# One gather ahead of the overflow loop, the last expert's weights loaded early, and one memory's keys and values moved into the first mixture's tail

## The chip, the cores and the metric

The kernel runs on one core of a Trainium2 chip. The metric is the device time of one execution in microseconds (us), as the median of the runs. A matrix product runs on TensorE (PE), elementwise work on VectorE (DVE), ScalarE (ACT) and GpSimd (POOL). SyncE (SP) issues the plain DMA loads, and POOL issues the indirect ones (gathers and scatters by a list of rows). Each engine works through its own instructions in order, and they wait for one another by semaphores.

## The reference

Two blocks of two layers each work on 512 tokens of width 1024. The change touches the second block only. Each of its two layers mixes the tokens, normalises, sends each token to 2 of 16 experts, and normalises again:

```python
def memory_branch(mq, mem, w_mem_kv):          # mem: 256 x 1024, w_mem_kv: 1024 x 1024
    kv = jnp.einsum('bmd,de->bme', mem, w_mem_kv)
    mk, mv = jnp.split(kv, 2, axis=-1)         # 4 heads of 128
    ...
    s = jnp.einsum('bshd,bmhd->bhsm', q, mk) * (MEM_HEAD_DIM ** -0.5)
    p = jax.nn.softmax(s, axis=-1)
    return jnp.einsum('bhsm,bmhd->bshd', p, mv)

def second_block(x, mem, ...):
    for l in range(DEPTH):
        mix = token_mixing(x, mem, ...)        # pooling, sparse attention, memory_branch
        x = layer_norm_2(DN_ALPHA_2 * x + mix, ln1_g[l], ln1_b[l])
        ffn = moe(x, w_router, router_bias, w1[l], w3[l], w2[l])
        x = layer_norm_2(DN_ALPHA_2 * x + ffn, ln2_g[l], ln2_b[l])
    return x
```

In `moe` an expert computes `(silu(xb @ w1[e]) * (xb @ w3[e])) @ w2[e]` for its tokens (1024 to 512 to 1024), and a token's two results are added with their gate weights. All is fp32. The memory is the same in both layers; only its weight matrix differs, so the keys and values of layer 1 hang on nothing that layer 0 computes.

## The kernel before, in words

**Products.** An fp32 product is made of three passes (`mm3`, lines 368 to 370: hi by hi, lo by hi or hi by lo, hi by lo) over operands that `split` (L374 on ACT, L376 on DVE) has cut into a rounded part hi and a rest lo. A weight tile of 128 x 2048 or 128 x 1024 is loaded by SP (L2011), split, and used. A few products whose operands are plain fp32 go through PE whole, as one `matmul` (L1478, L1881).

**The mixture.** `route` ranks the tokens of each expert by products with a triangular matrix, and makes for each expert a list of 96 slots (`SLOTS`; `slots`, L1709 and L1710). POOL gathers the 96 rows of an expert from `xd` in DRAM (`gather`, L1720), with up to four experts fetched ahead (`AHEAD`). PE turns them (`turn`, L1731), the first two products give `a` (tiles HP, `Ha`, L1756), and `down` turns `a` (tiles YP, L1765, cut into `Yhi` and `Ylo`) and multiplies it with w2. POOL scatters the rows to `yd` in DRAM (L1791). An expert with more than 96 tokens takes further blocks in a loop whose count is read at run time (`overflow`, `For_i` at L1907); all engines pass this loop's head, and with the inputs here its body is not run. Before the loop stand, on POOL, the gathers of experts 0 to 3 and a scatter of zeros into the rows of the last expert. The first `turn` comes after the loop.

**The tail of a mixture.** The last expert is not scattered: its product stays on the chip (`both`), and a one-hot matrix `own` carries it to the tokens. For each of four groups of 128 tokens `stats(t)` sums on PE the residual `h[t]` (through the identity, L1881, whole fp32, two products of 128 x 512) and the last expert's rows (L1883, four products), and DVE takes mean and variance (L427). POOL and DVE have added the scattered rows (`yd`, read by SP at L1853) to `h[t]` before (L1868 on POOL, L1870 on DVE, eight each). Then comes the norm: a power on POOL (L384), ACT L445, DVE L446, POOL L448. SP's order here is written out: the eight reads of `yd`, then the last expert's w2 (`wide<-in_wmoed`, two loads of 1 MB), which take the place that earlier tiles leave.

**The start of the next mixing.** `memory_kv` loads the memory (1 MB) and its weights (eight loads of 512 KB), splits both, and makes keys (96 passes of 128 x 256) and values (48 passes of 128 x 512, tiles AP). ACT copies the values out (L1466). Then the tokens are turned (tiles IP, L464), cast and split, and the products with `xwin` begin. In layer 1 PE does all this between the tail of layer 0's mixture and the first product with `xwin`.

## Time and profile before

| | |
|---|---|
| median of 3 runs | 3015.38 us (3015.05 to 3016.5) |
| the profiled execution | 3014.35 us |
| its span, first to last instruction | 3012.6 us |
| PE busy | 2869.8 us, 95% of the span |
| DVE, ACT, POOL busy | 72%, 48%, 15% |
| mean granted TensorE clock | 0.976 of full speed |

The profile's page gives, for each engine, the time in which it was busy and its share of the span. PE is busy for nearly all of it, so what is left to gain or lose lies in the few places where it is idle or runs slowly, and these are read from the trace by time. Times in the trace count from the span's start. The first mixture runs from about 1800 to 2160, the second from about 2650 to the end.

### The profile page before, as it was taken

To read this page: it belongs to the slowest core of one execution; us is meant where nothing else is said; L and a number is where in the kernel's file an instruction comes from. 1 tells how busy PE (TensorE), PEld (TensorE's weight loads), DVE (VectorE), ACT (ScalarE), POOL (GpSimd) and SP (SyncE) were. 2 spreads that over 40 slices of the span, in tenths; PEclk is the share of its full clock that TensorE was granted. 3 is DMA by queue.
4 is the path that set the end of the run, shared out by engine and by line. 5 is a ranking of instruction groups with operands and counts; after the bars stand their busy time and mean duration, and the time that the engine had idled before them with its cause. 6 is when DMAs were issued, how large, how long until landed. Compare 5 with 4: busy or idle time off the path is not lost.

```text
span 3012.6 us, 38089 instructions
## 1 busy us (share of the span) xinstructions
PE 2869.8 (95%) x14030; PEld 2250.3 (75%) x14030; DVE 2174.2 (72%) x3477; ACT 1434.1 (48%) x2214; POOL 456.2 (15%) x443
## 2 busy tenths in 40 slices
PE   7999999999999999999999998999799999979995
PEld 6777888888678888878777775776587877857773
DVE  6998655666968555687965467999678764579996
ACT  4444432324444333345444325887345444248883
POOL 3412000013111000012001021110311010022103
PEclk9999999999999999999999998999799999989998
DMA  5121332342213322352222377995631322669983
GB/s 191 35 106 49 99 98 92 99 143 70 64 54 95 98 98 98 106 170 89 78 88 84 105 264 266 379 389 223 230 109 60 95 88 80 245 224 374 384 321 135
DMA packets 128655, 457.35 MB, mean 152 GB/s; under 512 B 15761, under 2 KB 16977, under 8 KB 127057
## 3 DMA queue, kind: packets, MB, share of 16 engines
q1 hardware_dynamic: 117840, 425.50, 40.2%
q0 software_dynamic: 7168, 16.79, 1.8%
q10 hardware_dynamic: 3456, 12.58, 1.0%
q8 instruction: 112, 1.84, 0.2%
q14 instruction: 79, 0.64, 0.1%
HBM read 429.12 MB, written 27.26 MB: 151 GB/s over the span
## 4 chain that ended last, share of the span: by engine, by line
PE 64%; DVE 7%; ACT 2%; DMA 2%; issue 1%; POOL 1%; POOLq 0%; SPq 0%; DVEq 0%; ACTq 0%; another core or an unknown queue 0%
PE AP L368 12%; PE AP L369 12%; PE AP L370 12%; PE HP L368 4%; PE HP L369 4%; PE HP L370 4%; PE YP L369 2%; PE YP L370 2%; PE YP L368 2%; PE BP L369 1%; PE BP L370 1%; PE BP L368 1%; DVE cacc L784 1%; DVE lo L376 1%; PE O L1569 1%
## 5 line engine op out<-in xcount | busy, mean ns | idle before, releaser
L368 PE MATMUL AP<-g,hi 128*128 128x512 f32 (+1 forms) x1888 | 728.2, 387 | 25.3 <-ACT wide L445 7.4
L369 PE MATMUL AP<-g,hi 128*128 128x512 f32 (+1 forms) x1888 | 721.9, 383 | 8.2 <-DVE g L376 8.2
L370 PE MATMUL AP<-g,lo 128*128 128x512 f32 (+1 forms) x1888 | 723.0, 383 | 0.0
L376 DVE TENSOR_TENSOR lo<-raw,hi 128x1024 fp32r<-128x1024 f32 x322 | 409.6, 1274 | 371.4 <-ACT hi L374 362.2
L374 ACT CAST hi<-raw 128x1024 fp32r<-128x1024 f32 x334 | 350.1, 1051 | 581.9 <-PE AP L369 386.4
L368 PEld LDWEIGHTS AP<-g,hi 128*128 128x128 f32 x1888 | 360.3, 191 | 97.2 <-ACT wide L445 7.6
L369 PEld LDWEIGHTS AP<-g,hi 128*128 128x128 f32 x1888 | 360.4, 191 | 75.6 <-DVE g L376 9.2
L370 PEld LDWEIGHTS AP<-g,lo 128*128 128x128 f32 x1888 | 360.5, 191 | 67.5 <-issue 2.6
L376 DVE TENSOR_TENSOR lo<-g,hi 128x1024 fp32r<-128x1024 f32 x204 | 238.9, 1217 | 23.3 <-ACT hi L374 22.9
L376 DVE TENSOR_TENSOR lo<-wide,hi 128x1024 fp32r<-128x1024 f32 x188 | 221.9, 1225 | 40.7 <-ACT hi L374 40.5
L374 ACT CAST hi<-g 128x1024 fp32r<-128x1024 f32 x204 | 206.9, 1049 | 50.0 <-PE AP L370 32.5
L374 ACT CAST hi<-wide 128x1024 fp32r<-128x1024 f32 x188 | 190.6, 1048 | 47.8 <-DMA wide<-in_wmoed 26.8
L369 PE MATMUL HP<-lo,Txt 128*96 128x512 f32 x512 | 203.3, 397 | 0.8 <-DVE lo L376 0.6
L368 PE MATMUL HP<-hi,Txt 128*96 128x512 f32 x512 | 200.9, 400 | 1.1 <-ACT Txt L374 1.1
L370 PE MATMUL HP<-hi,Txt 128*96 128x512 f32 x512 | 202.0, 394 | 0.0
L368 PE MATMUL AP<-hi,g 128*128 128x512 f32 x416 | 171.4, 416 | 0.3 <-DVE g L886 0.3
L370 PE MATMUL AP<-hi,g 128*128 128x512 f32 x416 | 164.2, 397 | 0.2 <-DVE g L891 0.2
L369 PE MATMUL AP<-lo,g 128*128 128x512 f32 x416 | 163.0, 393 | 0.0
L368 PE MATMUL BP<-hi,g 128*128 128x512 f32 x352 | 136.8, 390 | 0.0
L369 PE MATMUL BP<-lo,g 128*128 128x512 f32 x352 | 136.6, 389 | 0.0
L370 PE MATMUL BP<-hi,g 128*128 128x512 f32 x352 | 134.1, 389 | 0.0
L369 PEld LDWEIGHTS HP<-lo,Txt 128*96 128x96 f32 x512 | 83.0, 162 | 39.8 <-DVE lo L376 4.1
(490 smaller groups left out, 4934.8 us busy)
## 6 DMA issues: line engine op xcount, KB each, us to landing
wide<-in_wmoeu SPq DMA_DIRECT2D x64, 1024.0 KB, 8.6
g<-in_wmoeu SPq DMA_DIRECT2D x64, 1024.0 KB, 8.6
raw<-in_wup SPq DMA_DIRECT2D x88, 512.0 KB, 3.5
g<-in_wmoed SPq DMA_DIRECT2D x34, 1024.0 KB, 9.1
wide<-in_wmoed SPq DMA_DIRECT2D x30, 1024.0 KB, 9.7
raw<-in_xwin SPq DMA_DIRECT2D x50, 512.0 KB, 3.7
raw<-in_xgate SPq DMA_DIRECT2D x48, 512.0 KB, 3.6
raw<-in_wdown SPq DMA_DIRECT2D x44, 512.0 KB, 3.5
```

The costliest lines, as they stand in the source:

```text
L368: mm(ps, a[0], b[0], start=start, stop=False)
L369: mm(ps, a[0], b[1], start=False, stop=False)
L370: mm(ps, a[1], b[0], start=False, stop=stop)
L374: self.nc.scalar.copy(hi, src)
L376: (engine or self.nc.vector).tensor_tensor(out=lo, in0=src, in1=hi.bitcast(F32), op=OP.subtract)
L784: ve.scalar_tensor_tensor(acc, ubs[c][:, j:j + S], w_dw[:, 31 * c + j:31 * c + j + 1], acc, op0=OP.mult, op1=OP.add)
L1569: nc.tensor.matmul(O[j][64 * b:64 * b + 64, t * 128:(t + 1) * 128], v[:, s, c:c + 64], PT[i - 1 + b][:, s, :], start=s == 0, stop=s == t, ...
```

## The change

Three things change.

First, in both mixtures only the gather of expert 0 stands ahead of the overflow loop. The zero tile, the gathers of experts 1 to 3 and the scatter of zeros come after it. The loop's count is computed directly from the ranks (`more`: for each expert, which of the thresholds in `past` its count exceeds), and read earlier.

Second, in both mixtures the last expert's w2 is loaded ahead of the reads of `yd`, and is split into tiles of its own (`apart`), so that its products can come ahead of the sums.

Third, the memory's keys and values of layer 1 are computed in the tail of layer 0's mixture, by whole fp32 products without splits (`memory_whole`): keys 32 products of 128 x 256, values 16 of 128 x 512. `memory_kv` at the start of layer 1's mixing is gone.

```diff
@@ route
+        nx, xs, xe = t16("nx"), t16("xs"), t16("xe")
+        more = self.pp.tile([128, 16, 5], F32, name=f"more{l}")
+        tt(more, rk[:, 4, :].unsqueeze(2).to_broadcast([128, 16, 5]), self.past.unsqueeze(1).to_broadcast([128, 16, 5]),
+           OP.is_gt)
+        blocks = L.s([128, 1])
+        ve.tensor_reduce(out=blocks, in_=more, op=OP.add, axis=AX.XY)
+        n = self.pp.tile([128, 1], I32, name=f"nblk{l}")
+        ve.tensor_copy(n, blocks)
+        n = nc.values_load(n[0:1, 0:1], min_val=0, max_val=2 * S // (SLOTS + 1))
...
-        cnt = L.s([128, 16])
-        ve.tensor_copy(cnt, rk[:, 4, :])
...
-        ve.tensor_scalar(nx, cnt, SLOTS + 0.5, None, op0=OP.is_gt)
-        for c in range(2 * SLOTS, S, SLOTS):
-            stt(nx, cnt, c + 0.5, nx, op0=OP.is_gt, op1=OP.add)
+        ve.reduce_sum(out=nx, in_=more, axis=AX.X)
...
-        ve.tensor_copy(n, xe[:, 15:16])
@@ mixing
-        raw = self.g8(shape=(128, 8, 256))
-        nc.sync.dma_start(raw, self.A["mem"])
-        kv = self.memory_kv(A, l, raw)
+        if l == 0:
...
+            kv = self.memory_kv(A, l, raw)
+        else:
+            kv = self.kv
@@ new
+    def memory_fetch(self, l, part):
...
+        ws = [self.g8(shape=(128, 2, D)) for _ in range(2)]
...
+        if part == 0:
+            mem = self.g8(shape=(128, 8, 256))
+            nc.sync.dma_start(mem, self.A["mem"])
+        for i, w in enumerate(ws):
+            at = 4 * part + 2 * i
+            nc.sync.dma_start(w, self.A[f"wmem{l}"][at:at + 2].rearrange("o p n -> p o n"))
...
+    def memory_whole(self, lanes, keys, values, kv):
...
+        for h, u in enumerate(us):
+            ps = lanes[h % 2].P((128, 256))
+            for k in range(8):
+                nc.tensor.matmul(ps, u[:, k * 128:(k + 1) * 128], mem[:, k], start=k == 0, stop=k == 7)
+            nc.scalar.copy(mk[:, h], ps)
+            yield
...
+                for t in range(2):
+                    nc.tensor.matmul(vp[t], mem[:, k, t * 128:t * 128 + 128], u[:, j * 512:(j + 1) * 512],
+                                     start=k == 0, stop=k == 7)
+            yield
+        for t in range(2):
+            nc.scalar.copy(kv[:, 2 + t], vp[t])
@@ moe
-        for e in range(AHEAD):
-            self.gather(xg[e], idx, e)
+        self.gather(xg[0], idx, 0)
+        self.overflow(L, (T, H, Y), l, info)
...
-        nc.gpsimd.memset(zero, 0.0)
-        self.scatter(zero, idx, NE - 1, f"rows{l}")
-        self.overflow(L, (T, H, Y), l, info)
+        with self.tc.issue_after(nc.gpsimd.memset(zero, 0.0).ins):
+            for e in range(1, AHEAD):
+                self.gather(xg[e], idx, e)
+            self.scatter(zero, idx, NE - 1, f"rows{l}")
...
+        ds_.apart = True
+        last_units = [ds_.next() for _ in range(4)]
+        cut = self.cut
+        keys = values = None
+        if not last:
+            keys = self.memory_fetch(l + 1, 0)
...
-        self.down(Y, ds_.next, a, idx, NE - 1, parts)
+        self.down(Y, iter(last_units).__next__, a, idx, NE - 1, parts)
+        product = self.product
...
-        add(0)
-        add(1)
+        add(0, cut)
+        add(1, cut)
         add(2, self.added)
-        now = stats(0)
+        fill = iter(())
+        if not last:
+            self.kv = self.g8()
+            fill = self.memory_whole((L, Y), keys, lambda: self.memory_fetch(l + 1, 1), self.kv)
+        with self.tc.issue_after(product.ins):
+            next(fill, None)
+            now = stats(0)
         add(3, self.known_x)
         for t in range(NT):
+            next(fill, None)
             then = stats(t + 1) if t + 1 < NT else None
...
+        for _ in fill:
+            pass
@@ Stream.next
+        if self.apart:
+            both = net.g8(FR, (128, 2, 1024))
+            hi, lo = both[:, 0], both[:, 1]
```

On POOL, at the loop of the first mixture, these are the rows before. `g_14881` and `g_14883` are the tiles of the gathered rows, `nblk` is the loop's count, and L1907 is the loop.

```order
L1826 MEMSET zero_15063 96x1024
L1720 DMA g_14881<-xd,slots_15011 96x1024 x2
L1720 DMA g_14883<-xd,slots_15011 96x1024 x2
L1791 DMA yd<-zero_15063,slots_15011 1024x1024
L1906 TENSOR_LOAD nblk_15049
L1907 COMPARE_AND_BRANCH
```

And now; the loop is L1967 here, and its body lies between the two parts.

```order
L1763 DMA g_14883<-xd,slots_15036 96x1024
L1699 TENSOR_LOAD nblk_14984
L1967 COMPARE_AND_BRANCH
```

```order
L1870 MEMSET zero_15253 96x1024
L1763 DMA g_14883<-xd,slots_15036 96x1024
L1763 DMA g_14885<-xd,slots_15036 96x1024 x2
L1834 DMA yd<-zero_15253,slots_15036 1024x1024
```

One indirect DMA is left ahead of the loop, and four are behind it.

On SP, at the end of the first mixture, the rows before. `yd` are the scattered rows, `in_wmoed` the last expert's w2, `in_wmem` and `in_mem` the memory's weights and the memory.

```order
L1853 DMA wide_17931<-yd 128x1024 x2
L1853 DMA wide_17934<-yd 128x1024 x2
L1853 DMA wide_17937<-yd 128x1024 x2
L1853 DMA wide_17940<-yd 128x1024 x2
L2011 DMA wide_17954<-in_wmoed 128x2x1024
L2011 DMA wide_17979<-in_wmoed 128x2x1024
L2011 DMA raw_18188<-in_wmem 128x1024
L410 DMA g_18003<-in_ln_rows 128x2048
L1264 DMA g_18143<-in_mem 128x2048
```

And now:

```order
L2072 DMA wide_17931<-in_wmoed 128x2x1024
L2072 DMA wide_17939<-in_wmoed 128x2x1024
L1481 DMA g_17949<-in_mem 128x2048
L1484 DMA g_17947<-in_wmem 128x2x1024
L1484 DMA g_17948<-in_wmem 128x2x1024
L2072 DMA raw_18266<-in_xwin 128x1024
L1904 DMA wide_17953<-yd 128x1024 x2
L1904 DMA wide_17956<-yd 128x1024 x2
L1904 DMA wide_17959<-yd 128x1024 x2
L1904 DMA wide_17962<-yd 128x1024 x2
L410 DMA g_18005<-in_ln_rows 128x2048
```

Five loads and one of `xwin` moved ahead of the reads of `yd`; the two loads with the weights of the values follow behind L410.

On PE, behind the last expert's turned `a` (L1765 before, L1808 now), before the change: the sums of the first two groups, then w2 (tile `YP_17953`).

```order
L1765 MATMUL YP_17944<-c_ident,Ha_17920 128x96 x4
L1881 MATMUL HP_18027<-g_14420,c_ident 128x512
L1881 MATMUL TP_18023<-g_14420,c_ident 128x512
L1881 MATMUL HP_18050<-g_14420,c_ident 128x512
L1881 MATMUL TP_18046<-g_14420,c_ident 128x512
L368 MATMUL YP_17953<-hi_17956,Yhi_17949 96x512
```

And now: four products of w2 by `Yhi`, then those that also use `Ylo`, and behind all 24 of them the keys (L1495) and the first group's sums (L1933 and L1935).

```order
L1808 MATMUL YP_17966<-c_ident,Ha_17920 128x96 x4
L368 MATMUL YP_17975<-g_17933,Yhi_17971 96x512
L369 MATMUL YP_17975<-g_17933,Yhi_17971 96x512
L368 MATMUL YP_17990<-g_17941,Yhi_17971 96x512
L369 MATMUL YP_17990<-g_17941,Yhi_17971 96x512
L370 MATMUL YP_17975<-g_17933,Ylo_17972 96x512
```

```order
L1495 MATMUL LP_18026<-g_17949,g_17947 128x256 x8
L1495 MATMUL YP_18059<-g_17949,g_17947 128x256 x8
L1495 MATMUL LP_18095<-g_17949,g_17948 128x256 x7
L1933 MATMUL HP_18040<-g_14422,c_ident 128x512
L1933 MATMUL TP_18036<-g_14422,c_ident 128x512
L1935 MATMUL TP_18036<-g_17965,own_17924 128x512 x2
```

The sums moved from ahead of w2 to behind it and behind 23 of the 32 products of the keys. The last key products, the other groups' sums and, at the end, the 16 products of the values (L1504) follow.

## Rows read from the trace of the kernel before

**Rows 1.** The page, part 1: busy us, share of the span, instructions.

```profile
PE 2869.8 (95%) x14030; PEld 2250.3 (75%) x14030; DVE 2174.2 (72%) x3477; ACT 1434.1 (48%) x2214; POOL 456.2 (15%) x443
```

**Rows 2.** The chain that ended last, 1810 to 1840: start, us, what.

```profile
1815.42 0.32 POOL g L1720
...
1820.76 4.85 DMA yd<-zero,slots
...
1827.24 1.54 PE TP L1731 x8
...
1833.86 0.33 PE TP L1731 x4
```

**Rows 3.** Timeline of the second mixture's loop: start, us, engine, line, tile, [idle before].

```profile
2665.27 1.10 POOL L1720 DMA_INDIRECT g<-xd,slots  x1 [11.92 <-DVE nx L1690]
...
2677.49 0.42 PE L1731 MATMUL TP<-c_ident,g 96*128 96x96 f32 x1 [10.38 <-DVE Ls L1846]
```

**Rows 4.** Timeline, the last scatter of layer 0 and the SP read that waits for it.

```profile
2104.06 0.91 POOL L1791 DMA_INDIRECT yd<-y,slots  x1 [9.73 <-ACT y L1786]
...
2107.72 4.08 SPq L1853 DMA_DIRECT2D wide<-yd  x8
```

**Rows 5.** Timeline, a small DVE reduction in the routing.

```profile
1812.28 0.21 DVE L1666 TENSOR_REDUCE keep<-room 128x4 f32<-128x64 f32 x1
```

**Rows 6.** DMA issues, 1811 to 1830: count and median us from issue to landing.

```profile
g<-xd,slots POOLq DMA_INDIRECT x5, 6.4
```

**Rows 7.** Windows: us, busy us by engine, granted clock, DMA share, GB/s.

```profile
2080.00:2095.00 15.00, 14.90 (x67) 10.15 (x66) 14.06 (x15) 13.69 (x18) 1.18 (x1) 1.00 0.01 3
```

**Rows 8.** Timeline of the first mixture's tail.

```profile
2108.96 0.39 PE L370 MATMUL HP<-hi,Txt 128*96 128x512 f32 x1
...
2111.90 1.45 SPq L2011 DMA_DIRECT2D wide<-in_wmoed  x2
...
2123.97 1.99 ACT L374 CAST hi<-wide 128x1024 fp32r<-128x1024 f32 x2 [12.77 <-DMA wide<-in_wmoed]
...
2133.72 0.40 PE L370 MATMUL YP<-hi,Ylo 128*96 128x512 f32 x1
...
2138.83 2.77 POOL L384 TENSOR_TENSOR Hs<-Hs,mhalf 128x1 f32<-128x1 f32 x1 [15.47 <-DVE Hs L383]
...
2159.20 1.27 POOL L448 TENSOR_TENSOR g<-wide,g 128x512 f32<-128x512 f32 x1 [0.69 <-DVE mb L1414]
```

**Rows 9.** The chain: a whole fp32 product 128x512, one pass, two whole 128x256.

```profile
2130.72 0.86 PE YP L1881 x2
2131.57 0.23 PE YP L369
...
1377.05 0.86 PE IP L1478 x4
```

**Rows 10.** Timeline, from the values' copies to the first full `xwin` product, layer 1.

```profile
2181.24 1.28 ACT L1466 COPY g<-AP 128x512 f32<-128x512 f32 x2 [0.76 <-PE AP L370]
...
2186.24 0.58 ACT L374 CAST g<-IP 128x512 fp32r<-128x512 f32 x1 [1.26 <-PE IP L464]
...
2186.62 0.50 PE L369 MATMUL AP<-g,hi 128*128 128x512 f32 x1 [0.42 <-DVE g L376]
```

**Rows 11.** Windows in the first mixture's tail, columns as in Rows 7.

```profile
2125.00:2130.00 5.00, 4.41 (x11) 2.74 (x12) 4.74 (x5) 4.01 (x5) 0.00 (x0) 0.56 1.03 423
2130.00:2135.00 5.00, 5.00 (x22) 3.41 (x21) 3.23 (x4) 2.47 (x4) 0.00 (x0) 1.00 0.80 256
```

**Rows 12.** Timeline of the second mixture's tail.

```profile
2959.00 0.40 PE L370 MATMUL HP<-hi,Txt 128*96 128x512 f32 x1
...
2961.54 11.92 POOL L1868 TENSOR_TENSOR g<-g,wide 128x512 f32<-128x512 f32 x8 [6.51 <-DMA wide<-yd]
...
2986.82 0.68 DVE L427 BATCH_NORM_STATS2 Hs<-HP 128x6 f32<-128x512 f32 x1
...
2988.91 1.02 POOL L384 TENSOR_TENSOR Hs<-Hs,mhalf 128x1 f32<-128x1 f32 x1 [15.45 <-DVE Hs L383]
```

More of the change, by code (lines that the diff above doesn't have):

```diff
@@ L369, in mm3 @@
         mm(ps, a[0], b[1], start=False, stop=False)
-        mm(ps, a[1], b[0], start=False, stop=stop)
+        self.product = mm(ps, a[1], b[0], start=False, stop=stop)
     def split(self, hi, lo, src, engine=None, after=None):
@@ L375, in split @@
         with self.tc.issue_after(after.ins) if after else nullcontext():
-            (engine or self.nc.vector).tensor_tensor(out=lo, in0=src, in1=hi.bitcast(F32), op=OP.subtract)
+            self.cut = (engine or self.nc.vector).tensor_tensor(out=lo, in0=src, in1=hi.bitcast(F32), op=OP.subtract)
     def rsqrt(self, L, v, n, scale=1.0, add=EPS):
@@ L1200, in block2_consts @@
             nc.sync.dma_start(self.rb, bass.AP(tensor=src.tensor, offset=src.offset, ap=[[0, 128], [1, 16]]))
+            self.past = self.blk.tile([128, 5], F32, name="past")
+            nc.vector.tensor_scalar(self.past, self.iota[:, 1:6], float(SLOTS), 0.5, op0=OP.mult, op1=OP.add)
             self.rank = self.blk.tile([128, 2, 4], F32, name="rank")
@@ L1261, in mixing_ @@
         kept = lambda tag, n=512: self.pp.tile([128, n], F32, tag=tag, bufs=1, name=self.nm(tag))
-        raw = self.g8(shape=(128, 8, 256))
-        nc.sync.dma_start(raw, self.A["mem"])
-        kv = self.memory_kv(A, l, raw)
+        if l == 0:
+            raw = self.g8(shape=(128, 8, 256))
+            nc.sync.dma_start(raw, self.A["mem"])
+            kv = self.memory_kv(A, l, raw)
+        else:
+            kv = self.kv
         self.flush(I)
@@ L1467, in memory_kv @@
         return kv
+    def memory_fetch(self, l, part):
+        nc = self.nc
+        ws = [self.g8(shape=(128, 2, D)) for _ in range(2)]
+        mem = None
+        if part == 0:
[4 more added lines that the diff above has]
+            nc.sync.dma_start(w, self.A[f"wmem{l}"][at:at + 2].rearrange("o p n -> p o n"))
+        return [w[:, i] for w in ws for i in range(2)], mem
+    def memory_whole(self, lanes, keys, values, kv):
+        nc = self.nc
+        us, mem = keys
+        mk = kv[:, 0:2].rearrange("p a (b c) -> p (a b) c", b=2)
+        for h, u in enumerate(us):
[4 more added lines that the diff above has]
+            yield
+        us, _ = values()
+        vp = [L.P() for L in lanes]
+        for kp, u in enumerate(us):
+            for j in range(2):
+                k = 2 * kp + j
+                for t in range(2):
[4 more added lines that the diff above has]
+            nc.scalar.copy(kv[:, 2 + t], vp[t])
     def memory(self, L, kv, queries, br):
@@ L1647, in route @@
             mm(rk[:, t + 1:5], self.one_r, both[:, t:t + 1].to_broadcast([128, 4 - t, 16]), start=False, stop=t == NT - 1)
+        t16 = lambda name: self.pp.tile([128, 16], F32, name=f"{name}{l}")
+        nx, xs, xe = t16("nx"), t16("xs"), t16("xe")
[7 more added lines that the diff above has]
+        n = nc.values_load(n[0:1, 0:1], min_val=0, max_val=2 * S // (SLOTS + 1))
         X, W = ([part(NT, 16) for _ in range(2)] for part in (exact, room))
@@ L1684, in route @@
         idx = idx, self.weights(Tw, 16)
-        cnt = L.s([128, 16])
-        ve.tensor_copy(cnt, rk[:, 4, :])
-        t16 = lambda name: self.pp.tile([128, 16], F32, name=f"{name}{l}")
-        nx, xs, xe = t16("nx"), t16("xs"), t16("xe")
-        ve.tensor_scalar(nx, cnt, SLOTS + 0.5, None, op0=OP.is_gt)
-        for c in range(2 * SLOTS, S, SLOTS):
-            stt(nx, cnt, c + 0.5, nx, op0=OP.is_gt, op1=OP.add)
+        ve.reduce_sum(out=nx, in_=more, axis=AX.X)
         ve.tensor_tensor_scan(xe, self.ones[:, 0:16], nx, 0.0, op0=OP.mult, op1=OP.add)
@@ L1696, in route @@
         ve.memset(ctr, 0.0)
-        n = self.pp.tile([128, 1], I32, name=f"nblk{l}")
-        ve.tensor_copy(n, xe[:, 15:16])
         return idx, (E, g, r, xs, xe, ctr, n)
@@ L1905, in overflow @@
         E, g, r, xs, xe, ctr, n = info
-        rv = nc.values_load(n[0:1, 0:1], min_val=0, max_val=2 * S // (SLOTS + 1))
-        with self.tc.For_i(0, rv, 1):
+        with self.tc.For_i(0, n, 1):
             a, sel = L.s([128, 16]), L.s([128, 16])
@@ L1999, in __init__ @@
         self.net, self.src, self.base, self.wide, self.i = net, src, base, wide, 0
-        self.slow, self.pairs = (), []
+        self.slow, self.pairs, self.apart = (), [], False
     def fetch(self, n):
@@ L2034, in next @@
         self.i += 1
-        hi = net.ringp.tile([128, 1024], FR, tag="hi", name=net.nm("hi"))
-        lo = net.ringp.tile([128, 1024], FR, tag="lo", name=net.nm("lo"))
+        if self.apart:
+            both = net.g8(FR, (128, 2, 1024))
+            hi, lo = both[:, 0], both[:, 1]
+        else:
+            hi = net.ringp.tile([128, 1024], FR, tag="hi", name=net.nm("hi"))
+            lo = net.ringp.tile([128, 1024], FR, tag="lo", name=net.nm("lo"))
         net.split(hi, lo, raw, net.nc.gpsimd if self.i in self.slow else None, after)
```

## The prediction

> **What bounds the kernel now.** I read the page first. PE is busy for 95% of the span [rows 1], so a gain can only come from the places where PE stands idle or runs at the low clock. The chain of waits and the timeline show three such places that the diff touches.
>
> The first is the overflow loop of each mixture. The gather of expert 0 is issued at 1815.42. PE's first turn of its rows comes at 1827.24, and what ends the wait is not that gather: it is the landing of the zero scatter, the fifth indirect DMA in a row, issued at 1820.76 and 4.85 us long [rows 2]. The second mixture has the same picture, 2665.27 to 2677.49 [rows 3].
>
> The second is the tail of each mixture. PE ends the last expert's first products at 2108.96; SP issues the last w2 only at 2111.90, behind the reads of `yd`, and ACT waits for it until 2123.97, 12.77 us [rows 8]. In between PE has only four sums to do. The second mixture does the same with its own first products ending at 2959.00 [rows 12].
>
> The third follows the first tail: the sums and the norm leave PE little to do, and then the memory's keys and values of layer 1 run. The first full `xwin` product comes at 2186.62, some 78 us after 2108.96 [rows 8, 10].
>
> **The loop.** Ahead of the gather DVE now has four more small operations (the comparison, two reductions, a cast). A small reduction takes 0.21 us [rows 5]; with the wider operands I take 1.0 us in all, so the gather goes out at 1816.42. What a gather alone takes is not shown, but a scatter alone is: issued at 2104.06, and the read that waits for it goes out at 2107.72, 3.66 us later [rows 4]. From the landing to PE's first turn the trace has 1827.24 - (1820.76 + 4.85) = 1.63 us [rows 2]. So the turn comes at 1816.42 + 3.66 + 1.63 = 1821.7, 5.5 us earlier. In the second mixture it is 2665.27 + 6.29 = 2671.6 against 2677.49, 5.9 us. Together **11.4 us**. The other bound is the median of the gathers there, 6.4 us, with several in flight [rows 6]: then 2 x 2.7 less, 6.0 us. I take 3.66, since nothing else is in flight.
>
> The three other gathers go out after the loop, behind the zero tile's memset: the first at about 1822.6, landed by 1829.0 at 6.4 us. The turn that needs it stood at 1833.86 [rows 2]; it moves 5.5 us earlier, but now lies 16 passes of 0.23 us further back in PE's order, so about 1832. That hides it with 3 us to spare; without the cover PE would wait for what exceeds it.
>
> **The tails, last w2.** The DMA engines are at rest before the tail: 0.01 of their time from 2080 to 2095, at full PE [rows 7]. So the two loads of w2, the memory and the first 2 MB of its weights can land there, if SP gets their places; by the order of the tiles these are freed when expert 14's weights are cut, before 2095. Then ACT and DVE cut w2 around the last first-products, and `down` waits only for its own turned operand. `Yhi` comes at about 2111.2, and `Ylo` at about 2113.8, since two cuts of w2 and the making of `own` stand ahead of it on DVE. Four products run before it, 20 after it: 2113.8 + 20 x 0.23 [rows 9] = 2118.4, against 2133.72 + 0.23 [rows 8].
>
> In the second mixture nothing more lies between. Its first products end 850.0 us later [rows 8, 12], so `down` ends at about 2968.5. The first two groups' sums are interleaved there: four whole products at 0.86 and eight passes at 0.23, 5.3 us, which ends at 2973.8. Before, the first mean and variance from these sums began at 2986.82. Thus **13.0 us**. What is late next is POOL: its eight additions take 11.92 us from 2961.54, to 2973.5 [rows 12], and the power for the first group follows them. It would start at 2973.8 + 2.1 = 2975.9 in any case, so POOL has 2 us to spare. From there to the end the norm's work is unchanged.
>
> **The memory in the first tail.** By rows a whole 128 x 512 product costs 0.86 us, one of 128 x 256 costs 0.43 (two in 0.86, four records), and a pass of three 0.23 [rows 9]. The keys cost 32 x 0.43 = 13.8 us and the values 16 x 0.86 = 13.8. After 2118.4 PE does 23 key products (9.9, to 2128.3), the first sums (two whole products and four passes, 2.64, to 2130.9), a key product and three more sums (8.4), eight key products (3.4, to 2142.7), and the values (13.8, to 2156.5). Then come the values' copies on ACT (1.28) and eight casts of the turned tokens at 0.58 [rows 10]: the first full `xwin` product at 2162.4 instead of 2186.62, **24.2 us** for both edits in this tail.
>
> The norm must not be late. It took from 2138.83 (the first power) to 2160.47, 21.6 us [rows 8], partly beside splits of the memory that are gone. With the first sums at 2130.9 the power comes near 2133, and even at 21.6 us its end is 2154.6, under the values. If that cover is gone, each us counts. POOL's additions end before the first sums, as their `yd` reads are no longer followed by 2 MB of w2.
>
> A rule speaks against this edit. One row shows a whole product at 0.86 us, against 3 x 0.23 = 0.69 for the three passes [rows 9]. The Trainium skill ("FP8 and Floating Point Precision", TensorE Precision Notes) states that true fp32 makes four passes through the array; at 0.23 a pass that is an estimate of 0.92, and by it the values and keys together would cost 29.4 us and not 27.5, the gain 1.9 less. The edit thus buys PE time for the splits it drops on ACT and DVE; it pays here because the tail had PE idle.
>
> **The clock.** After the wait for w2 PE ran 2125 to 2130 at 0.56 of its clock, and at 1.00 in the next 5 us [rows 11]. In the new tails PE has waits of 1 to 2 us around the turn of `a` and `Ylo`. If the clock falls once there and ten passes run at the low level, they cost 2.3 us more in each tail, 4.6 in both. That is one bound and nothing the other; I take half, 2.3 us in all.
>
> **Sum.** 11.4 + 13.0 + 24.2 = 48.6, less 2.3 for the clock, 46.3 us. Against the profiled execution, 3014.35 - 46.3 = 2968.0. The median of the runs lies 1.0 us above that execution, so **2969 us**.
>
> **Rivals.**
>
> *The loop's wait is not the zero scatter alone.* If the gather lands as slowly alone as among others, or expert 1's rows come late and PE, in order, waits for them, the loops give 0 to 6 us of the 11.4: 2974 to 2980. For it: the gather then has nothing after it that hides it. Against it: no DMA stands behind it.
>
> *The last w2 is not early.* SP works in order; if a place for w2 or the memory frees only when the last expert's own products have read it, SP stands there, and the reads of `yd` behind it stand too. Then 5 MB arrive as late as 2 MB did, `down` is where it was in both tails. What remains is the loops' 11.4 and what the stretch from `down`'s end to `xwin` loses: 52.7 us before (2133.95 to 2186.62) against 44.0 in the working above (2118.4 to 2162.4), 8.7. That is 20.1 us, 2995. Against it: the tiles' order, and idle DMA engines at 2080.
>
> *The norm chain takes over in the first tail.* The keys stand ahead of the first sums. If the norm takes more than 23.5 us from 2133, its last additions come after the values, and `xwin` waits. At 29.5 us that is 6 us, 2975. For it: ACT's casts of w2 and copies of keys share its engines. Against it: splits of the memory no longer do.
>
> *The clock falls at `Ylo` and stays low through the tails (the other side).* For it: PE was busy for 4.4 of 5 us at 0.56 [rows 11]. At the low level every product takes twice as long: `down` to 2122.4, the 23 keys to 2142.2, sums and keys to 2171.0, values to 2198.5, `xwin` at 2204.4, 17.8 us later than before. The second tail would gain 3.5 us and the loops 11.4: 2.9 us slower, 3018. It decides only if the clock stays low for nearly the whole 43 us of products; if for half of them, the sum is still 23 us faster. Against it: as the passes of w2 went on, the next stretch had 1.00 [rows 11].
> The Trainium skill ("TensorE: Matmul & The Clock Gate", HAM oscillation) tells of waits between bursts of matmuls that put the array back to half rate, so that the next burst starts slow; the trace agrees (0.56 after the wait for w2).
>
> *It does not do what it says:* the loop's head waits for other landings, and the memory's work only changes places: 3012 to 3016.
>
> **How the numbers follow.** Forecast 0.61; slow loop 0.14; late w2 0.07; norm chain 0.07; low clock 0.05; no effect 0.03; a new wait that no row of before can show, and that costs more than all of it saves, 0.03. This kernel's measurement tells a change from none at about 0.2%, 6 us. Faster by more than that: the first four, 0.89, and of the low clock 0.02 where it recovers halfway, 0.91. Within: no effect and the rest of the low clock, 0.06. Slower: the new wait, 0.03. The forecast's own range is 2964 to 2975. The range reaches down to 2958, for a gather as quick as 3 us and a norm chain shorter by the splits that are gone (DVE's and ACT's eight each no longer beside it), and up to 2986, over the slow loop and a clock that recovers halfway through one tail; late w2, the low clock, no effect and the new wait stay out, 0.18.
>
> **What would show it.** From the first gather on POOL to PE's first turn some 6 us instead of 11.8; ACT without a wait for `in_wmoed` in the tails; PE busy from 2113.8 on, with 23 key products before the first sums; `xwin`'s first full product some 53 us after the last first-product instead of 78; the first power of the second tail 17 us after its first products, not 30. Wrong would make it: a new wait of PE for a gather at expert 1, a wait of SP between w2 and `yd`, or a granted clock near 0.5 in the values' products.

## The result and the profile after

The changed kernel takes 2973.22 us (median of 4 runs, 2967.93 to 2975.52), the kernel before 3015.94 beside it. The ratio is 0.9858, with a 95% interval of 0.9845 to 0.987: 43 us or 1.4% less, where 46 were forecast. The profiled execution took 2971.21 us with a span of 2969.3, 43.3 less than before.

The page, part 1, as in [rows 1]:

```profile
PE 2864.6 (96%) x13982; PEld 2242.9 (76%) x13982; DVE 2164.5 (73%) x3460; ACT 1424.0 (48%) x2202; POOL 463.2 (16%) x443
```

PE's busy time fell by 5.2 us against [rows 1], so about 38 of the 43 us are idle time of PE that is gone.

The loop in the first mixture, first the chain (start, us, what), then the timeline of POOL and PE, and the second mixture's timeline. They answer to [rows 2, 3]:

```profile
1812.11 0.43 PE LP L1686
...
1817.71 4.35 DMA g<-xd,slots
...
1823.15 1.52 PE TP L1774 x8
```

```profile
1817.71 1.24 POOL L1763 DMA_INDIRECT g<-xd,slots  x1 [13.68 <-DVE slots L1753]
...
1823.13 1.54 PE L1774 MATMUL TP<-c_ident,g 96*128 96x96 f32 x8 [3.52 <-DVE Ls L1891]
...
1833.28 0.85 PE L1774 MATMUL TP<-c_ident,g 96*128 96x96 f32 x8
```

```profile
2638.14 1.10 POOL L1763 DMA_INDIRECT g<-xd,slots  x1 [13.39 <-DVE slots L1753]
...
2643.71 1.54 PE L1774 MATMUL TP<-c_ident,g 96*128 96x96 f32 x8 [3.64 <-DVE Ls L1891]
```

From the gather's issue to PE's first turn 5.42 and 5.57 us now, against 11.82 and 12.22. What ends the wait is the gather itself, no longer the scatter of zeros. The turn of expert 1 at 1833.28 stands without a wait, so the first gather behind the loop is in time; PE waits for none of the other two either (its longest wait from there to 1900 is 0.3 us).

The first tail, timeline, as [rows 8, 10]:

```profile
2105.01 0.40 PE L370 MATMUL HP<-hi,Txt 128*96 128x512 f32 x1
...
2107.75 0.47 PE L368 MATMUL YP<-g,Yhi 128*96 128x512 f32 x1 [0.58 <-ACT Yhi L1815]
...
2110.14 0.47 PE L370 MATMUL YP<-g,Ylo 128*96 128x512 f32 x1 [1.22 <-DVE Ylo L1816]
...
2114.84 3.62 PE L1495 MATMUL LP<-g,g 128*128 128x256 f32 x16
2118.29 3.62 PE L1495 MATMUL YP<-g,g 128*128 128x256 f32 x16
...
2124.77 1.02 PE L1933 MATMUL HP<-g,c_ident 128*128 128x512 f32 x2
...
2152.16 1.02 PE L1504 MATMUL YP<-g,g 128*128 128x512 f32 x2
...
2159.35 0.50 PE L369 MATMUL AP<-g,hi 128*128 128x512 f32 x1
```

No wait for `in_wmoed` is left. PE goes from w2's products to 23 key products and then to the sums; from 2105.01 to the first full `xwin` product it is 54.34 us, where it was 77.66.

The second tail, timeline, as [rows 12], then where w2's products end there, and windows (columns as [rows 7]; the first is of the first tail):

```profile
2926.39 0.40 PE L370 MATMUL HP<-hi,Txt 128*96 128x512 f32 x1
2928.00 0.55 PE L1808 MATMUL YP<-c_ident,Ha 96*128 96x96 f32 x4 [1.21 <-DVE Ha L1799]
...
2929.46 15.33 POOL L1920 TENSOR_TENSOR g<-g,wide 128x512 f32<-128x512 f32 x8 [6.53 <-DMA wide<-yd]
...
2931.52 0.74 PE L370 MATMUL YP<-g,Ylo 128*96 128x512 f32 x1 [1.18 <-DVE Ylo L1816]
...
2945.60 1.02 POOL L384 TENSOR_TENSOR Hs<-Hs,mhalf 128x1 f32<-128x1 f32 x1 [0.81 <-DVE Hs L383]
```

```profile
2938.69 1.02 PE L1933 MATMUL HP<-g,c_ident 128*128 128x512 f32 x2
```

```profile
2110.00:2115.00 5.00, 4.86 (x21) 3.49 (x22) 0.83 (x2) 0.69 (x1) 4.84 (x5) 1.00 1.02 401
...
2929.13:2930.11 0.98, 0.98 (x4) 0.56 (x4) 0.98 (x5) 0.00 (x0) 0.65 (x1) 1.00 0.97 343
2930.12:2930.34 0.22, 0.21 (x1) 0.00 (x0) 0.22 (x1) 0.00 (x0) 0.22 (x1) 0.50 0.96 372
2930.00:2935.00 5.00, 3.82 (x10) 2.33 (x9) 4.96 (x5) 0.00 (x0) 4.92 (x3) 0.51 0.99 383
```

The waits for `Ylo` are alike (1.22 and 1.18 us), but the clock stayed at 1.00 in the first tail and fell in the second. It fell at 2930.11, while PE was still on the fourth product of w2 and 0.2 us before the wait for `Ylo` began; the waits ahead of that, 1.21 us for `Ha` and 0.58 for `Yhi`, are the same in both tails. In the second tail the first power comes 19.2 us after the last first-product (29.9 before), and the end 42.9 us after it (53.6 before).

### The profile page after: what moved, and what is told of

Read it like the earlier page. It is cut to its first block, busy times and chain, and to the rows that moved or that the text cites. A ratio compares the mean times of both kernels' runs of the same rounds, so it can differ in the third digit from the quotient of the medians.

```text
span 2969.3 us, 37938 instructions
## 1 busy us (share of the span) xinstructions
PE 2864.6 (96%) x13982; PEld 2242.9 (76%) x13982; DVE 2164.5 (73%) x3460; ACT 1424.0 (48%) x2202; POOL 463.2 (16%) x443
## 4 chain that ended last, share of the span: by engine, by line
PE 66%; DVE 7%; ACT 1%; issue 1%; POOL 1%; DMA 0%; POOLq 0%; DVEq 0%; ACTq 0%
PE AP L368 12%; PE AP L369 12%; PE AP L370 12%; PE HP L370 4%; PE HP L369 4%; PE HP L368 4%; PE YP L370 2%; PE YP L369 2%; PE YP L368 2%; PE BP L370 1%; PE BP L368 1%; PE BP L369 1%; DVE cacc L784 1%; PE O L1610 1%; DVE lo L376 1%
## 5 line engine op out<-in xcount | busy, mean ns | idle before, releaser
L368 PE MATMUL AP<-g,hi 128*128 128x512 f32 (+1 forms) x1856 | 718.1, 388 | 14.1 <-ACT Mw L711 4.0
L369 PE MATMUL AP<-g,hi 128*128 128x512 f32 (+1 forms) x1856 | 711.9, 384 | 8.1 <-DVE g L376 8.1
L370 PE MATMUL AP<-g,lo 128*128 128x512 f32 (+1 forms) x1856 | 712.4, 384 | 0.0
L376 DVE TENSOR_TENSOR lo<-raw,hi 128x1024 fp32r<-128x1024 f32 x314 | 400.2, 1276 | 363.2 <-ACT hi L374 354.2
L374 ACT CAST hi<-raw 128x1024 fp32r<-128x1024 f32 x326 | 341.6, 1050 | 575.6 <-PE AP L369 382.9
L368 PEld LDWEIGHTS AP<-g,hi 128*128 128x128 f32 x1856 | 353.0, 190 | 86.2 <-ACT Mw L711 4.4
L369 PEld LDWEIGHTS AP<-g,hi 128*128 128x128 f32 x1856 | 353.7, 191 | 75.3 <-DVE g L376 9.2
L370 PEld LDWEIGHTS AP<-g,lo 128*128 128x128 f32 x1856 | 353.2, 190 | 67.2 <-issue 2.6
L376 DVE TENSOR_TENSOR lo<-wide,hi 128x1024 fp32r<-128x1024 f32 x180 | 212.4, 1226 | 25.4 <-ACT hi L374 25.2
L374 ACT CAST hi<-wide 128x1024 fp32r<-128x1024 f32 x180 | 182.7, 1050 | 22.2 <-PE HP L370 19.1
L368 PE MATMUL AP<-hi,g 128*128 128x512 f32 x400 | 165.0, 416 | 0.3 <-DVE g L886 0.3
L370 PE MATMUL AP<-hi,g 128*128 128x512 f32 x400 | 157.8, 397 | 0.2 <-DVE g L891 0.2
L384 POOL TENSOR_TENSOR Bs<-Bs,mhalf 128x1 f32<-128x1 f32 x8 | 7.8, 977 | 687.2 <-DVE Bs L383 687.2
```

The costliest lines, as they stand in the source:

```text
L368: mm(ps, a[0], b[0], start=start, stop=False)
L369: mm(ps, a[0], b[1], start=False, stop=False)
L370: self.product = mm(ps, a[1], b[0], start=False, stop=stop)
L374: self.nc.scalar.copy(hi, src)
L376: self.cut = (engine or self.nc.vector).tensor_tensor(out=lo, in0=src, in1=hi.bitcast(F32), op=OP.subtract)
L384: self.nc.gpsimd.tensor_tensor(out=r, in0=x, in1=self.mhalf[:, 0:n], op=OP.pow)
```

## The experiments

All start from the changed kernel, but for one. "Over" and "under" are differences of the ratios to the kernel before, times 3015; the changed kernel stands at 0.9858. Single executions of one kernel differ by up to 12 us, so stages are read from the traces.

**loop_five_ahead**: all gathers and the scatter of zeros ahead of the loop again, with the early count.

```diff
-        self.gather(xg[0], idx, 0)
-        self.overflow(L, (T, H, Y), l, info)
...
+        for e in range(AHEAD):
+            self.gather(xg[e], idx, e)
...
+        self.scatter(zero, idx, NE - 1, f"rows{l}")
+        self.overflow(L, (T, H, Y), l, info)
```

Expected: 

> The changed kernel, but with all four gathers and the scatter of zeros ahead of the overflow loop again; the count of blocks is still made early. Theory (the loop's head waits for the last indirect DMA issued, so what counts is how many stand in the row): from the first gather to the first turn about 11.8 us in both mixtures again instead of 5.4 and 5.6, and the time about 12 us over the changed kernel, 2983 to 2987 us. Rival (the early count is what helps): as the changed kernel, 2971 to 2976 us.

Measured: 2983.03 us, ratio 0.9899 (0.9882 to 0.9915), 12 us over. Gather to turn 11.32 and 12.30 us. The early count alone brings nothing; the theory holds.

**loop_four_ahead**: four gathers ahead, only the zeros behind.

```diff
-        self.gather(xg[0], idx, 0)
+        for e in range(AHEAD):
+            self.gather(xg[e], idx, e)
         self.overflow(L, (T, H, Y), l, info)
...
-        with self.tc.issue_after(nc.gpsimd.memset(zero, 0.0).ins):
-            for e in range(1, AHEAD):
-                self.gather(xg[e], idx, e)
-            self.scatter(zero, idx, NE - 1, f"rows{l}")
+        nc.gpsimd.memset(zero, 0.0)
+        self.scatter(zero, idx, NE - 1, f"rows{l}")
```

Expected: 

> The changed kernel, but with the four gathers ahead of the overflow loop and only the scatter of zeros behind it. Theory (what counts is the place of the last DMA in the row): the fourth gather is issued 4.1 us after the first, so gather to turn is about 4.1 + 4.4 + 1.1 = 9.6 us, the time about 8 us over the changed kernel, 2980 to 2983 us. Rival (only the scatter's write of zeros is slow): gather to turn 5.5 to 6.5 us, the time within 2 us of the changed kernel.

Measured: 2985.62 us, ratio 0.9907 (0.9888 to 0.9925), 15 us over and not to be told from five. Gather to turn 10.29 and 11.74 us. Its chain:

```profile
1820.75 4.82 DMA g<-xd,slots
1825.57 1.39 issue
1826.96 1.54 PE TP L1774 x8
```

The fourth gather lands 4.82 us after its issue, as late as the zeros did in [rows 2]. The place of the last DMA in the row counts, whether it is a gather or the zeros. A gather among others also lands later than one alone: 4.82 us here and 6.17 in the second loop, against 4.35 and 4.23. So 8 us were expected, and the two loops of the traces hold 11.

**loop_only**: the kernel before with the loop's part alone (the tails' parts undone).

Expected: 

> The kernel before, with the change in the loop alone: early count and one gather ahead of the overflow loop; w2 and the memory as before. Theory (the loops' stalls stand apart from the tails): 10 to 12 us under the kernel before, 3003 to 3006 us, gather to first turn 5.4 to 5.6 us. Rival (PE needs the head start of the loads that the stall gave): less than 8 us under, 3007 us or more.

Measured: 3009.57 us (10 runs, 3005.54 to 3015.53), ratio 0.9981 (0.9972 to 0.9991): 5.7 us under the kernel before, 2.7 to 8.4; the medians alone are 7.3 apart. The profiled execution, 3005.54, was the fastest of the ten. In it gather to turn is 5.57 and 5.39 us; as the gather itself goes out some 0.9 us later than before, 11.4 us are saved from the last product of the ranks to the turn in both loops, and the span is 9.1 us shorter. By the median the number is the rival's, by the loops' stages the theory's. Why the other runs lose more stays open, and with it whether PE needs the head start that the stall gave to the loads.

**w2_late**: the last w2 behind the reads of `yd`, cut into the tiles that all experts use in turn (the ring).

```diff
-        ds_.apart = True
-        last_units = [ds_.next() for _ in range(4)]
...
-        self.down(Y, iter(last_units).__next__, a, idx, NE - 1, parts)
+        self.down(Y, ds_.next, a, idx, NE - 1, parts)
...
```

Expected: 

> The changed kernel, but with the last expert's two loads of w2 behind the reads of yd again, and its parts in the ring as before. The memory's loads stay ahead of the reads, the key products behind down's products as far as the order has it. Theory (PE waits for these loads in both tails): the second tail is 10.7 us longer again, the first loses about 12 to 15 us, the time 23 to 26 us over the changed kernel, 2996 to 3000 us. Rival (the memory's products fill the first tail's wait, so w2 counts only in the second): about 11 us over, 2983 to 2986 us.

Measured: 2999.9 us, ratio 0.9955 (0.9941 to 0.9969), 29 us over. The first tail takes 69.99 us, the second's end 56.7. PE's wait in the first tail, then the second tail's timeline:

```profile
PE YP L368 <- ACT hi L374: 14.8, 1, 14.8
```

```profile
2957.20 0.74 PE L368 MATMUL YP<-hi,Yhi 128*96 128x512 f32 x1 [14.13 <-ACT hi L374]
...
2974.38 1.02 POOL L384 TENSOR_TENSOR Hs<-Hs,mhalf 128x1 f32<-128x1 f32 x1 [18.49 <-DVE Hs L383]
```

PE waits for these loads in both tails, as the theory says, but its range was 3 us too small: the second tail cost 13.8 us and not 10.7. The load itself is no later there than in the kernel before: PE's first product of w2 comes 15.9 us after the last first-product (2941.35), against 16.3. But the first sums, which the kernel before has ahead of w2, stand behind w2's products here, and the first power comes 33.0 us after the last first-product instead of 29.9.

**w2_late_keys_free**: w2_late, with the first keys and sums allowed ahead of w2.

```diff
-        with self.tc.issue_after(product.ins):
-            next(fill, None)
-            now = stats(0)
+        next(fill, None)
+        now = stats(0)
```

Expected: 

> The kernel with w2 behind the reads of yd, but with the first key products and the sums not held back behind down's products: in PE's order 8 key products and four sums stand ahead of w2's. Theory (PE has too little to do ahead of w2; what is late is w2 and all that hangs on it): first tail at most 3 to 5 us shorter than with w2 late, second tail unchanged, 2995 to 2998 us. Rival (it is only the order that keeps PE idle in the first tail): the first tail as in the changed kernel, 2984 to 2986 us.

Measured: 2988.92 us, ratio 0.9914 (0.9897 to 0.993), 17 us over. The first tail is 62.51 us, 7.5 shorter than in w2_late:

```profile
PE YP L368 <- ACT hi L374: 4.0, 1, 4.0
```

Neither number was right: work that hangs on nothing late shortens the wait from 14.8 to 4.0 us, which is half of what the early load brings in this tail. The second tail, expected to be unchanged, is 2.8 us shorter (53.9), since there too the first sums stand ahead of w2 again. So part of what w2_late lost was the order and not the load.

**memory_old**: keys and values at the start of the mixing again, in three passes.

```diff
-        if l == 0:
...
-            kv = self.memory_kv(A, l, raw)
-        else:
-            kv = self.kv
+        raw = self.g8(shape=(128, 8, 256))
+        nc.sync.dma_start(raw, self.A["mem"])
+        kv = self.memory_kv(A, l, raw)
...
```

Expected: 

> The changed kernel, but with the second memory's keys and values at the start of layer 1's mixing again, in three passes with splits. Theory (down ends early, then the stretch from down's end to the first xwin product is 52.7 us as before instead of 44.5): about 8 us over the changed kernel, 2980 to 2983 us. Rival (whole products cost PE as much as the removed passes and stalls): within 2 us of the changed kernel.

Measured: 2987.03 us, ratio 0.9907 (0.9891 to 0.9924), 15 us over where 8 were expected. The first tail is 69.00 us. PE's waits in it, and one window:

```profile
PE AP L368 <- ACT wide L445: 4.9, 1, 4.9
PE AP L369 <- DVE g L376: 4.3, 2, 3.9
PE AP L368 <- ACT g L374: 4.2, 2, 2.1
```

```profile
2145.00:2150.00 5.00, 4.40 (x21) 4.40 (x22) 3.10 (x6) 1.70 (x3) 2.68 (x2) 0.52 0.90 333
```

With w2 early PE reaches the memory's products sooner, and then stands for the norm, for splits of the memory, and runs slowly after it. From the end of w2's products to `xwin` it takes 12 us longer than in the changed kernel, not 8; the other 2.5 us of this tail come from w2's products, most of which ran at the low clock here and none in the changed kernel's first tail.

**whole_old_place**: whole products, but at the old place.

```diff
         else:
-            kv = self.kv
+            kv = self.g8()
+            for _ in self.memory_whole((A, A), self.memory_fetch(l, 0), lambda: self.memory_fetch(l, 1), kv):
+                pass
...
```

Expected: 

> The changed kernel, but with the memory's whole products, loads and all, at the start of layer 1's mixing instead of in the tail. Theory (the splits of the memory and its weights on ACT and DVE, beside the norm, are what made the old place dear once w2 came early): most of the 14 us that the old place cost comes back, from the last first-product to xwin 56 to 60 us, the time 2 to 6 us over the changed kernel, 2975 to 2979 us. Rival (the place is what counts, since these products stand behind the sums in PE's order): from the last first-product to xwin 65 us or more, 11 us or more over the changed kernel, 2984 us or more.

Measured: 2983.48 us, ratio 0.9891 (0.9876 to 0.9907), 10 us over. The first tail is 69.09 us, the same as with three passes and splits. The theory fell, and the rival has it, 1 us short of its number. Timeline of PE:

```profile
2130.65 3.66 PE L1497 MATMUL AP<-g,g 128*128 128x256 f32 x16
...
2141.76 6.69 PE L1497 MATMUL AP<-g,g 128*128 128x256 f32 x16 [7.45 <-ACT wide L445]
...
2148.83 3.62 PE L1497 MATMUL AP<-g,g 128*128 128x256 f32 x16
```

The second head's keys need nothing of the norm, and still wait 7.45 us for ACT's L445, which reads the sums of the tail. That fits a wait for an accumulator that the sums still hold; in the tail the keys use other accumulators, those of the groups L and Y. No run here changed the accumulators alone.

**ylo_first**: the one-hot matrix ahead of the last first-products, the fourth cut of w2 behind `Ylo`.

```diff
+            if e == NE - 1:
+                own = ...
             nxt = self.up(H, unit, xt, *((down,) if e == NE - 1 else ()))
...
-        last_units = [ds_.next() for _ in range(4)]
+        last_units = [ds_.next() for _ in range(3)]
```

Expected: 

> The changed kernel, but with the one-hot matrix made before the last expert's first products and the fourth cut of w2 behind Ylo, so that Ylo waits on DVE for one cut less and for no one-hot matrix. Theory (PE's wait of 1.2 to 1.9 us for Ylo costs itself and lets the clock fall in the second tail, 2.3 us more): Ylo 1.5 to 2 us earlier, granted clock 1.00 through both tails, first tail 1 to 2 us shorter; in the second the additions on POOL are the next to be waited for, so only 1 us there; the time 2 to 3 us under the changed kernel, 2970 to 2971 us. Rival (the clock falls whatever the wait): no shorter second tail, within 1 us of the changed kernel.

Measured: 2972.31 us, ratio 0.9859 (0.9844 to 0.9874), no change: the first tail is 1.1 us shorter, the second's end 3.3 longer. `Ylo` was earlier and the clock stayed at 1.00 up to 9 us after the last first-product in both tails. But DVE, in order, came to the fourth cut only after an addition that waited for `yd`, and PE then waited 4.1 us for that cut. `yd` was late too: with the one-hot matrix early the last scatter went out 0.2 us after the last first-product, instead of 4.4 before it (DVE's timeline):

```profile
2922.11 1.21 DVE L376 TENSOR_TENSOR g<-wide,g 128x1024 fp32r<-128x1024 f32 x1
2923.35 0.56 DVE L1816 SCALAR_TENSOR_TENSOR Ylo<-YP,Yhi 128x384 fp32r<-128x384 f32 x1
2928.52 0.69 DVE L1923 TENSOR_TENSOR g<-g,wide 128x512 f32<-128x512 f32 x1 [4.61 <-DMA wide<-yd]
...
2930.80 2.28 DVE L376 TENSOR_TENSOR g<-wide,g 128x1024 fp32r<-128x1024 f32 x1
```

**ylo_first_less_pool**: the same, with the second tail's last two additions on POOL moved to DVE.

Expected: 

> As ylo_first, and in the second tail the fourth group's two additions on POOL go to DVE. Theory (POOL's 15.3 us of additions hold the first power): the first power 3 to 4 us earlier than in the changed kernel, and the end with it; the time 4 to 6 us under the changed kernel, 2967 to 2969 us. Rival (DVE, which makes the mean and variance, becomes the later of the two): the end no earlier than in ylo_first.

Measured: 2970.25 us, ratio 0.9851 (0.9837 to 0.9865), not to be told from either. The first power comes 22.49 us after the last first-product, as in ylo_first (22.47), though POOL stood idle 4.27 us before it. POOL was not what held it.

**own_early**: the one-hot matrix early, all cuts ahead of `Ylo`. **own_early_less_pool**: the same with the additions moved.

Expected: 

> The changed kernel, but with the one-hot matrix made before the last expert's first products; all four cuts of w2 stay ahead of Ylo. Theory (in ylo_first the fourth cut fell behind additions that wait for yd, and PE waited for it; with only the one-hot matrix moved, Ylo comes 0.8 us earlier and nothing gets later): PE's wait for Ylo about 0.5 us shorter in both tails, the time 1 to 3 us under the changed kernel, 2970 to 2972 us, more if the clock then holds in the second tail. Rival (the wait stays and the clock falls all the same): within 1 us.

Expected: 

> As own_early, and in the second tail the fourth group's two additions on POOL go to DVE. Theory (POOL and DVE each take longer while the other adds, and POOL's eight additions are as late as the first sums): POOL done 4 us earlier, the first power 1 to 3 us earlier than in own_early; the time 2968 to 2971 us. Rival (DVE is the later one): as own_early or 1 us over it.

Measured: 2979.65 us, ratio 0.9884 (0.9867 to 0.99), 8 us over, and 2976.48, 0.9871 (0.9855 to 0.9888), 4 us over. Both theories fell. With the additions moved POOL is done 5.0 us earlier in the second tail, and the first power is no earlier (21.5 us after the last first-product in both): PE waits there 4.2 us for an addition on DVE. In own_early the wait for `Ylo` fell to 0.4 us, and the first tail grew to 58.59 us. POOL's timeline in that tail, and in the changed kernel:

```profile
2104.41 3.02 POOL L1834 DMA_INDIRECT yd<-y,slots  x1 [15.10 <-ACT y L1829]
2113.81 12.35 POOL L1921 TENSOR_TENSOR g<-g,wide 128x512 f32<-128x512 f32 x7 [6.38 <-DMA wide<-yd]
```

```profile
2100.64 0.91 POOL L1834 DMA_INDIRECT yd<-y,slots  x1 [9.76 <-ACT y L1829]
2107.88 13.33 POOL L1920 TENSOR_TENSOR g<-g,wide 128x512 f32<-128x512 f32 x8 [6.33 <-DMA wide<-yd]
```

The last scatter comes 1.15 us after the last first-product (2103.26) instead of 4.37 before it, as ACT's two copies of those rows moved back in its order. The first read of `yd` comes 7.6 us later than in the changed kernel, and POOL's additions with it.

**own_behind_ylo**: the one-hot matrix right behind `Ylo`, nothing else.

```diff
         self.down(Y, iter(last_units).__next__, a, idx, NE - 1, parts)
+        own = ...
+        with self.tc.issue_after(self.low.ins):        # self.low: the instruction that makes Ylo
+            for t in range(NT):
+                ve.tensor_scalar(own[:, t], ...)
```

Expected: 

> The changed kernel, but with the one-hot matrix made right behind Ylo instead of ahead of it; the last expert's products, their places and the scatter ahead are untouched. Theory (own_early lost because making the matrix early put ACT's two copies of expert 14's rows, and with them the scatter, the reads of yd and the additions, 4 to 5 us later; Ylo itself was earlier and the wait shorter): the last scatter 4 to 5 us ahead of the last first-product as in the changed kernel, Ylo 0.8 us earlier, the tails 0.5 to 1 us shorter, 3 us more in the second if its clock then holds; 2969 to 2973 us. Rival (an earlier Ylo brings nothing, since the additions of yd are as late): the tails as in the changed kernel.

Measured: 2968.31 us (2961.65 to 2973.46), ratio 0.9845 (0.9828 to 0.9862): about 4 us under the changed kernel, though the intervals overlap. The profiled execution, 2961.65, is the fastest of five. Its trace shows the place: PE's wait, the window in the second tail, and POOL's timeline there:

```profile
PE YP L370 <- DVE Ylo L1816: 0.4, 1, 0.4
```

```profile
2925.00:2930.00 5.00, 5.00 (x22) 3.39 (x21) 4.86 (x8) 1.15 (x2) 4.84 (x4) 1.00 1.02 414
```

```profile
2923.20 11.21 POOL L1921 TENSOR_TENSOR g<-g,wide 128x512 f32<-128x512 f32 x6 [6.39 <-DMA wide<-yd]
2935.34 0.96 POOL L384 TENSOR_TENSOR Hs<-Hs,mhalf 128x1 f32<-128x1 f32 x1 [0.94 <-DVE Hs L383]
```

The wait is 0.4 us instead of 1.2, the clock is 1.00 there, the first power comes 15.1 us after the last first-product (2920.27) instead of 19.2, the end 39.6 instead of 42.9. The first tail is 0.7 shorter. Something else moved with the edit: POOL makes the first power behind six of its eight additions here, and behind all eight in the changed kernel, where they end 18.4 us after the last first-product. With all eight ahead, the power could not have come before about 18.4, so this order is part of the gain; no run separates it from the wait and the clock. It is the fastest version by the median.

## Why the prediction was right, step by step

*The loop, 11.4 us forecast.* From the last product of the ranks to the first turn the traces give 16.57 and then 11.02 us in the first mixture (1810.67 to 1827.24 before, 1812.11 to 1823.13 now), 5.5 saved, and 6.1 in the second: 11.6. The product of before, from its chain:

```profile
1810.67 0.44 PE LP L1645
```

The step was right in sum, with two terms off against each other: the gather took 4.35 us to land and not 3.66, and from there to the turn it was 1.07 and not 1.63. That the sum came out is in part luck. The rival with a slow gather was right by a quarter: 4.35 lies that far from 3.66 to the 6.4 that it took.

*The first tail, 24.2 forecast, 23.3 measured.* Against the last first-product every date was within 1 us of the working: `down` ended at 9.8 us (9.4 forecast), the keys at 19.8 (19.3), `xwin` at 54.3 (53.4). The whole products cost 0.43 us (eight keys in 3.45) and 0.86; the Trainium skill's four passes ("FP8 and Floating Point Precision", TensorE Precision Notes) would by an estimate at 0.23 a pass have made it 0.92, and the measured one is 3.7 passes of 0.23. The norm ended under the values, as forecast. The size has some luck in it, as the clock did not fall in this tail: in loop_five_ahead and loop_four_ahead, which have the same tails, it did, and the stretch took 55.9 and 56.6 us.

With neither of its two parts this stretch takes 77.7 us; with w2 early alone 69.0 (memory_old), with the memory's products in the tail alone 70.0 (w2_late), with both 54.3: 8.7 and 7.7 apart, 23.3 together. That looks as if the parts need each other, but w2_late_keys_free shows that it is mostly the order: with the keys and first sums ahead of the late w2 the memory's part alone brings 15.2 us (62.5), and 8.7 and 15.2 are 23.9. The prediction's rival on a late w2 put the loops and 8.7 us, 20 us in all, as what would remain of the whole; w2_late kept 14. The first tail's 7.7 is near its 8.7, but the second tail lost 3.1 us against the kernel before by the order, and this the rival did not have.

*The second tail, 13.0 forecast at full clock, 10.7 measured.* Two things took the difference, and one was not in the prediction. The first is the clock. From the first product that uses `Ylo` to the first sum PE took 7.17 us (2931.52 to 2938.69), where the first tail has 4.70 (2110.14 to 2114.84): 2.5 us. The prediction bounded this at 2.3 us a tail and took 2.3 for both; that one tail had it and the other not is luck.

The second is POOL, which was to have 2 us to spare. It had none: its eight additions took 15.33 us and not 11.92, and ended 18.4 us after the last first-product, 1.5 later than the 16.9 at which the working has the first power. In the changed kernel the slow clock hides this, as the sums come later still. In loop_four_ahead, whose tails are the same, w2's products end 1.9 us earlier in the second tail, and the first power then follows POOL's eighth addition without a gap, 18.4 us after the last first-product (2938.97):

```profile
2942.01 15.36 POOL L1919 TENSOR_TENSOR g<-g,wide 128x512 f32<-128x512 f32 x8 [6.49 <-DMA wide<-yd]
2957.33 1.03 POOL L384 TENSOR_TENSOR Hs<-Hs,mhalf 128x1 f32<-128x1 f32 x1
```

The end comes 42.0 us after the last first-product there, and in whole_old_place as well, against 42.9: so of the 2.3 us that are missing from 13.0 some 0.9 are the clock's, and the other 1.4, by this estimate, would stay at full clock as long as POOL makes its eight additions first. From the first power to the end it is 23.7 us, before and now, as forecast.

What makes the clock fall is not settled. Ten tails of the kept traces have `Ylo` at the place of the changed kernel, so that its first product comes 5.1 us after the last first-product (after, loop_five_ahead, loop_four_ahead, memory_old, whole_old_place). The clock fell in nine of them, in six 2.6 to 3.7 us after the last first-product, before PE's fourth product of w2 was done and so before any wait for `Ylo`, and in three at 5.6 to 5.7 us. In the ten tails where `Ylo` is earlier (ylo_first, own_early, both with the additions moved, own_behind_ylo) it did not fall in the first 9 us. So an earlier `Ylo` goes with a clock that holds, but why is open: the wait for `Ylo` alone cannot be the cause, since in six tails the clock was low before it, as in loop_five_ahead's second tail, whose fall comes 2.6 us after its last first-product (2936.60):

```profile
2937.00:2939.20 2.20, 0.55 (x4) 0.36 (x4) 2.20 (x3) 1.04 (x2) 0.00 (x0) 1.00 0.92 320
2939.25:2941.36 2.11, 2.01 (x4) 0.95 (x4) 2.11 (x7) 0.04 (x1) 1.82 (x1) 0.50 0.91 346
```

The Trainium skill's "TensorE: Matmul & The Clock Gate" (HAM oscillation) has waits between bursts put the array back to half rate; the traces agree in the second tail (0.51) and show in the first that equal waits can leave it at 1.00. The rival of a clock that stays low did not occur.

*The sum.* 11.6 + 23.3 + 10.7 = 45.6. The span fell by 43.3; 2.3 us more were spent outside these places (1.4 before the first routing, 1.2 in the second mixture's experts). That is within what two executions of one kernel differ by. But 0.8 of the 1.2 is clock behind the changed loop: the first 12 passes after the second turn took 5.24 us (2645.25 to 2650.49), against 4.48 before (2679.03 to 2683.51), and the prediction has no term for it.

## What to carry to other kernels

Ahead of a loop whose head waits for all that was issued, count the transfers in the row, not the one that the next work needs: the last one sets the time. Work that hangs on nothing belongs where PE waits, ahead in PE's order of all that waits; that it should have accumulators of its own is argued here and not tested. Before two changes are called worth more together than apart, look at the order in which each alone was tried. Waits of about one microsecond ahead of a train of products can cost PE 2.5 us more by the clock, and the same waits can cost nothing, so such a term belongs in a forecast as a range. And an engine whose work is counted as covered needs its price from rows in which the other engines are as busy beside it as they will be.

## What the runs showed of the hardware that was not expected

DVE and POOL slow each other, but not always both. In ylo_first the same cut of 128 x 1024 takes DVE 1.21 us while POOL has nothing to add, and 2.28 us at 2930.80, amid POOL's additions. In the changed kernel the same cut keeps its 1.22 us beside POOL, and it is POOL's addition that takes 3.74 us (2.87 at the same place of the first tail), where the later ones of [rows 12], with DVE idle beside them, take 1.26 each (timeline, 2929.4 to 2933.2):

```profile
2929.46 3.74 POOL L1920 TENSOR_TENSOR g<-g,wide 128x512 f32<-128x512 f32 x1 [6.53 <-DMA wide<-yd]
2929.78 1.22 DVE L376 TENSOR_TENSOR g<-wide,g 128x1024 fp32r<-128x1024 f32 x1
```

POOL's eight additions in the second tail grew from 11.92 us [rows 12] to 15.33 in the changed kernel, where DVE's cuts and additions lie beside them.

Two tails with the same waits, 1.2 us for `Ha`, 0.6 for `Yhi` and 1.2 for `Ylo`, had different ends: the clock stayed at 1.00 in one and fell to half in the other, and it fell before the last of these waits. Part of the spread between executions, 2967.93 to 2975.52 us at mean clocks of 0.986 to 0.981, goes with the clock.
